# Moving the return of the branches' parts from GpSimd's DMA queue to ScalarE's, one transfer a step

## The chip, the cores and the metric

The kernel runs on one core of a Trainium2 chip. The metric is the device time of one execution in microseconds (us). Three runs of the kernel before gave 2952.59, 2952.63 and 2953.83 us.

## The reference, cut to what matters

Two blocks run one after the other on a sequence of 512 rows of width 1024, in float32. The first is a recurrent layer and a mixture of 32 experts. The second has two layers, each of a feed-forward part, a mixer and another feed-forward part. Only the mixer is touched:

```
p = h @ w_in                                     # h: rmsnorm(x); 512 x (2560 + 3*1024)
gates = sigmoid(p[..., OFF_G:])                  # three gates of width 1024
y_f = fourier_mix(p[..., OFF_F:OFF_B], w_fourier)   # 4 groups of 128 -> 4 x 256
y_c = short_conv(...)                            # 512 -> 1024
y_p = pool_mix(p[..., OFF_P:OFF_G], w_pool, pool_scale)  # 4 groups of 128 -> 4 x 256
merged = gates[0]*y_f + gates[1]*y_c + gates[2]*y_p
x = x + merged @ w_o
```

In `fourier_mix` and in `pool_mix` each of four groups is first transformed along the sequence and then multiplied by a 128 x 256 matrix of its own. The transformed inputs of these products are the branches' parts.

## The kernel before, in words

Every float32 product is three TensorE matmuls (`mm3`, L241 to L243): each operand is a high part in float32r and a low part that holds the rest, and the products are high x high, high x low, low x high. ScalarE writes the high part of a weight block (`whi`, L192), VectorE the low part (`wlo`, L193). Weight blocks are prefetched by SyncE's queue (L157); some get a second block added on the way by an accumulating transfer of GpSimd's queue (L155). `Stream.advance` splits up to four blocks ahead; the tiles `whi` and `wlo` have five buffers each.

The mixer's product with `w_in` is done in groups (`group`), each of seven steps of 24 matmuls with 256 columns. After step i the group calls `todo[i]`, which runs one `tick`; a tick takes every job in the list `jobs` (Python generators) on by one `yield` and starts the new ones, and then `st.advance` prepares more weights. ScalarE reads PSUM after step 0 (L1486), step 1 (L1490), step 2 (L1496) and step 4 (L1505); VectorE reads the banks in `ends` (L1613 after step 3, L1610 after step 5, L1614 and L1615 after step 6). The order on every engine is the order of the program: an instruction that waits holds those behind it on the same engine.

In the first groups of a mixer the transformed inputs are made: `fourier` and `pool` end in `aside`, which splits them into a high and a low part and stores both in HBM (`keep_s`, L1720), as there is no room for them in SBUF. They return later. The last six groups of a mixer are named by g, in the order 4, 2, 3, 0, 1, 5. After each of the groups g = 2, 3, 0 and 1, TensorE does four small products of 512 columns, 12 matmuls, with the weights of `wbranch` and the two parts of group g that have come back: `BR[0]` (pool) and `BR[1]` (Fourier), each with a high and a low tile of 256 KB. The product i uses `BR[i % 2]`. The next group's steps follow on TensorE at once. The job `gates_pf` reads the four banks of the products in the next group (L1822 and L1823), after its steps 3 and 5.

Before the change `branches(g)` runs as one job after step 3 and issues all four transfers from GpSimd (L1838). In groups g = 2 and 3 a further `pool` job starts after step 1. There are four such groups in each of the two mixers, so eight sets of products and 32 transfers.

The tiles of `slot()` have 40 buffers under one tag; the four that a group's parts take are, from the second group on, those of the parts of the group before. In the program that the framework makes, the transfers of the two hardware queues (SyncE's and ScalarE's) share eight completion semaphores in turn, in program order: each waits, on its own engine, until the eighth such transfer before it has landed.

Of the kernel before, what the change touches and what calls it, by code (L numbers as in the profile page):

```python
# [10 lines left out]
F32 = mybir.dt.float32  # L11
# [226 lines left out]
def mm3(nc, ps, w, x, first, last, skip=False):  # L238

    (wh, wl), (xh, xl) = w, x  # L240
    nc.tensor.matmul(ps, wh, xh, start=first, stop=False, skip_group_check=skip)  # L241
    nc.tensor.matmul(ps, wh, xl, start=False, stop=False, skip_group_check=skip)  # L242
    nc.tensor.matmul(ps, wl, xh, start=False, stop=last, skip_group_check=skip)  # L243
# [1017 lines left out]
def dense_phase(K):  # L1261
    tc, A, C, st, X, vc, onesf, ident = (K[n] for n in ("tc", "A", "C", "st", "X", "vc", "onesf", "ident"))
    nc = tc.nc
# [9 lines left out]
    def bank():  # L1273
        return pp.tile([128, 512], F32, name="mm", tag="mm", bufs=6)
# [20 lines left out]
    def tmp(dt=F32):  # L1295
        return stage["pool"].tile([128, S], dt, name="t", tag="t", bufs=NT_F)
# [4 lines left out]
    def slot(x=False):  # L1301

        if x:
            return stage["pool"].tile([128, S], F32R, name="x", tag="x", bufs=4)
        return dp.tile([128, S], F32R, name="s", tag="s", bufs=40)
# [289 lines left out]
    def mixer(l, nxt):  # L1595
        nonlocal h
        keep, keep_s = K["keep"][l], K["keep_s"][l]
# [6 lines left out]
        def line(dt=F32):  # L1604
            return stage["pool"].tile([128, S + 16], dt, name="z", tag="z", bufs=2)
# [11 lines left out]
        def rows(todo, rstd=False, new=wide, margin=0):  # L1617

            t = {}

            def get(r):
                def f(make=False):
                    if make:
                        t[r] = new()
                        if margin:
                            V.memset(t[r][:, :, 0:margin], 0.0)
                            V.memset(t[r][:, :, S + margin:], 0.0)
                    v = t[r][:, :, margin:S + margin] if margin else t[r].rearrange("p (m x) -> p m x", m=2)
                    return v.rearrange("p m (t b) -> p m t b", t=2)
                return f  # L1630
            group(todo, rstd, quarters(get(0), get(1)))
            b = get(1)
            return t, lambda: TT(b()[:, :, 0], b()[:, :, 0], RB[0], op=OP.mult)
# [18 lines left out]
        def steps(**new):  # L1652
            return [lambda i=i: tick(new.get(f"s{i}", ())) for i in range(7)]
# [44 lines left out]
        for g in range(4):  # L1698
# [10 lines left out]
            else:  # L1709
                t = stage["pool"].tile([128, 2, S + 16], F32R, name="L", tag="L", bufs=2)  # L1710
# [5 lines left out]
        def aside(n, src, to=None):  # L1716

            t = yield from split(src, to)
            for i in range(2):
                nc.sync.dma_start(keep_s[2 * n + i], t[i].bitcast(F32))  # L1720
# [33 lines left out]
        def bc(t, i):  # L1754
            TT(t, t, conv[i], op=OP.mult)
            yield
            BC[i] = yield from split(t)

        def pool(t, i, to=None):
            half = 1 << i  # L1760
            w = 2 * half
            up = t[:, i // 2]
            s = [line() for _ in range(2)]
            cur, m = up, 1
            n = 0
            while m < w:
                nx = s[n % 2]
                ln = S + 16 - 2 * m + 1
                TT(nx[:, :ln], cur[:, 0:ln], cur[:, m:m + ln], op=OP.add)
                cur, m, n = nx, 2 * m, n + 1  # L1770
            win = cur[:, 8 - half:8 - half + S]
            yield
            t = tmp()
            act(t, win, AF.Copy, scale=1.0 / w)
            yield
            TT(t[:, 0:half], win[:, 0:half], edge[:, i, 0:half], op=OP.mult)
            if half > 1:
                TT(t[:, S - half + 1:], win[:, S - half + 1:], edge[:, i, 8:8 + half - 1], op=OP.mult)
            TT(t, t, up[:, 8:S + 8], op=OP.subtract)
            yield  # L1780
            yield from aside(4 + i, t, to)

        def once(f):
            f()
            yield 1
# [3 lines left out]
        p, f3 = rows(steps(s0=[once(f2), bc(b[0][:, :S], 0), bc(b[0][:, S:], 2)], s2=[bc(b[1][:, :S], 1)],  # L1789
                           s3=[bc(b[1][:, S:], 3)]), new=lines, margin=8)  # L1790
# [3 lines left out]
        spare = lambda: line(F32R)[:, :S]  # L1794

        def gates_c(t, f, i):

            f()
            act(t[0], t[0], AF.Sigmoid)
            yield  # L1800
            act(t[1], t[1], AF.Sigmoid)
            for r in range(2):
                v = t[r].rearrange("p (m x) -> p m x", m=2)
                if i:
                    nc.sync.dma_start(keep[4 + r:8:2].rearrange("m p x -> p m x"), v)
                    yield
                else:
                    for m in range(2):
                        G[2 * m + r] = v[:, m]

        def gates_pf(t, f, g, ps):

            f()
            act(t[0], t[0], AF.Sigmoid)
            yield
            act(t[1], t[1], AF.Sigmoid)
            yield
            for r in range(2):
                yield
                j = 2 * g + r  # L1820
                u, v = t[r][:, :S], t[r][:, S:]
                STT(u, ps[2 * r], vc("pscale", KD * l + j), u, op0=OP.mult, op1=OP.mult)  # L1822
                TT(v, v, ps[2 * r + 1], op=OP.mult)  # L1823
                if g < 2:
                    if r == 0:
                        Z["t"] = lines()
                    Z[j] = Z["t"][:, r, :S]
                    TT(Z[j], u, v, op=OP.add)
                else:
                    z = tmp()  # L1830
                    TT(z, u, v, op=OP.add)
                    nc.sync.dma_start(keep[8 + j], z)
                yield

        def back(n):
            t = slot(), slot()
            for i in range(2):
                nc.gpsimd.dma_start(t[i].bitcast(F32), keep_s[2 * n + i])  # L1838
            return t

        def load(n):
            g = dp.tile([128, S], F32, name="s", tag="s", bufs=40)
            nc.gpsimd.dma_start(g, keep[n])
            return g

        def loads(j):
            G[j], Z[j] = load(j), load(8 + j)

        BR = {}

        def branches(g):
            BR[0], BR[1] = back(4 + g), back(g)

        new = dict(s0=[once(f3), pool(p[0], 2)], s3=[pool(p[1], 3)])
        for n, g in enumerate((4, 2, 3, 0, 1, 5)):
            if g < 4:
                new["s3"] = [once(lambda: branches(g))]
                if n < 3:
                    new["s1"] = [pool(p[n - 1], n - 1, spare)]
            if g == 5:  # L1860
                loads(4)
                loads(5)
            t, f = rows(steps(**new))
            if g >= 4:
                new = dict(s0=[gates_c(t, f, 5 - g)])
                continue
            w = st.get(h)
            ps = [bank() for _ in range(4)]
            for i in range(4):
                sl = slice(128 * i, 128 * i + 128)  # L1870
                mm3(nc, ps[i], (w[0][:, sl], w[1][:, sl]), BR[i % 2], True, True)
            st.advance(h)
            h += 1
            new = dict(s0=[gates_pf(t, f, g, ps)])
# [109 lines left out]
    for l in range(L2):  # L1984
        ffn(prepper("gmix", l, prep_s), *[None, None] if l else [squares, None, gain("gffn1", 0)])
        close()
        mixer(l, lambda k: prep_s(k, gain("gffn2", l), True))
        if l + 1 < L2:
            ffn(prepper("gffn1", l + 1, prep_s), own=True)
            close()  # L1990
            open_ffn(3)
        else:
            ffn(last, None, tail, own=True)
# [150 lines left out]
```

## Time and profile before

| | |
|---|---|
| three runs, median | 2952.63 us |
| profiled execution | 2954.42 us |
| span of its trace | 2952.6 us |
| mean granted TensorE clock | 0.981 |
| TensorE matmuls busy | 2845.1 us (96% of the span) |
| VectorE busy | 2230.4 us (76%) |
| ScalarE busy | 1657.6 us (56%) |
| GpSimd busy | 403.7 us (14%) |

The profiled execution's time is 1.8 us over its span and 1.8 us over the median of the three runs. TensorE is busy nearly throughout, so a time can only fall where TensorE waits or runs at a lower clock.

### The profile page before, as it was taken

What the parts mean: (1) busy time and instruction counts of PE and PEld (TensorE: products, weight loads), DVE (VectorE), ACT (ScalarE), POOL (GpSimd) and SP (SyncE); (2) the same over time, 40 slices, a digit from 0 to 9 for tenths busy, and PEclk for the clock granted to TensorE, in tenths of its full rate; (3) what the DMA queues carried; (4) which work ended last, traced back from release to release, by engine and by line L of the source; (5) the groups of instructions that cost most, each with busy time, mean ns of one, the idle gap of its engine ahead of it and who ended that gap; (6) DMA issues with size and microseconds to landing.
All of it is one profiled execution on the core that took longest, in us unless ns stands there. A gap on an engine that the chain in (4) does not pass through costs nothing.

```text
span 2952.6 us, 44425 instructions
## 1 busy us (share of the span) xinstructions
PE 2845.1 (96%) x17882; PEld 2471.1 (84%) x17882; DVE 2230.4 (76%) x2778; ACT 1657.6 (56%) x2214; POOL 403.7 (14%) x371
## 2 busy tenths in 40 slices
PE   9997999999889999999899999999999998999998
PEld 7875676667558989998789999899899987899997
DVE  7688888898986758787678667777587876786674
ACT  4746888888764535654356344645356543563442
POOL 0034222220510000101110000100001011100002
PEclk9998999999999999999899999999999999999999
DMA  6374899999943545466644555465454676445551
GB/s 196 123 278 154 336 360 344 369 366 375 358 152 110 157 140 165 137 193 203 198 158 136 156 158 150 131 170 157 137 167 135 192 204 200 158 136 157 157 156 59
DMA packets 113889, 575.04 MB, mean 195 GB/s; under 512 B 13244, under 2 KB 23868, under 8 KB 61328
## 3 DMA queue, kind: packets, MB, share of 16 engines
q1 hardware_dynamic: 87536, 485.31, 44.9%
q0 software_dynamic: 25056, 85.82, 14.6%
q8 instruction: 141, 2.31, 0.3%
q10 hardware_dynamic: 1088, 1.05, 0.1%
q14 instruction: 68, 0.56, 0.1%
HBM read 549.37 MB, written 26.74 MB: 195 GB/s over the span
## 4 chain that ended last, share of the span: by engine, by line
PE 72%; DVE 4%; DMA 4%; ACT 2%; issue 1%; POOL 0%; POOLq 0%; SPq 0%; ACTq 0%; DVEq 0%
PE mm L242 14%; PE mm L243 14%; PE mm L241 14%; PE sv L241 8%; PE sv L243 8%; PE sv L242 8%; PE y L954 3%; DMA s<-branch 2%; DVE wlo L193 2%; PE h L919 2%; PE h L918 2%; ACT whi L192 1%; PE ht L932 1%; DMA rawg<-in_wblocks 1%; PE gat L889 1%
## 5 line engine op out<-in xcount | busy, mean ns | idle before, releaser
L241 PE MATMUL mm<-s,whi 128*128 128x256 f32 (+1 forms) x2262 | 744.6, 329 | 33.6 <-DMA s<-branch 31.4
L193 DVE TENSOR_TENSOR wlo<-raw,whi 128x1024 fp32r<-128x1024 f32 x493 | 606.7, 1240 | 221.5 <-ACT whi L192 221.4
L242 PE MATMUL mm<-s,whi 128*128 128x256 f32 (+1 forms) x2262 | 745.1, 329 | 5.8 <-DMA s<-branch 5.4
L243 PE MATMUL mm<-s,wlo 128*128 128x256 f32 (+1 forms) x2262 | 742.6, 328 | 0.0
L192 ACT ACTIVATE whi<-raw 128x1024 fp32r<-128x1024 f32 x495 | 513.2, 1051 | 156.5 <-PE mm L242 101.3
L241 PE MATMUL sv<-s,whi 128*128 128x256 f32 (+1 forms) x1912 | 544.3, 285 | 1.7 <-ACT sv L1486 1.7
L242 PE MATMUL sv<-s,whi 128*128 128x256 f32 (+1 forms) x1912 | 543.6, 284 | 0.0
L243 PE MATMUL sv<-s,wlo 128*128 128x256 f32 (+1 forms) x1912 | 543.5, 284 | 0.0
L241 PEld LDWEIGHTS mm<-s,whi 128*128 128x128 f32 x2262 | 430.4, 190 | 77.4 <-DMA s<-branch 18.8
L242 PEld LDWEIGHTS mm<-s,whi 128*128 128x128 f32 x2262 | 430.4, 190 | 51.9 <-DMA s<-branch 12.0
L243 PEld LDWEIGHTS mm<-s,wlo 128*128 128x128 f32 x2262 | 430.7, 190 | 38.6
L241 PEld LDWEIGHTS sv<-s,whi 128*128 128x128 f32 x1912 | 359.9, 188 | 4.5 <-ACT sv L1486 2.3
L243 PEld LDWEIGHTS sv<-s,wlo 128*128 128x128 f32 x1912 | 360.0, 188 | 2.2
L242 PEld LDWEIGHTS sv<-s,whi 128*128 128x128 f32 x1912 | 360.0, 188 | 2.1
L193 DVE TENSOR_TENSOR wlo<-rawf,whi 128x1024 fp32r<-128x1024 f32 x158 | 193.6, 1225 | 54.9 <-ACT whi L192 54.9
L193 DVE TENSOR_TENSOR wlo<-rawb,whi 128x1024 fp32r<-128x1024 f32 x162 | 200.1, 1276 | 22.4 <-ACT whi L192 20.3
L1592 DVE SCALAR_TENSOR_TENSOR X<-mm,X 128x512 f32<-128x512 f32 x95 | 65.5, 690 | 189.1 <-PE mm L243 189.0
L919 PE MATMUL h<-wlo,xt 128*64 128x512 f32 x512 | 196.2, 403 | 5.9 <-DVE wlo L193 5.1
L192 ACT ACTIVATE whi<-rawf 128x1024 fp32r<-128x1024 f32 x158 | 165.4, 1049 | 53.0 <-PE mm L242 33.9
L155 POOL DMA_DIRECT2D rawg<-in_wblocks x63 | 54.6, 867 | 986.4 <-DVE wlo L193 433.0
L918 PE MATMUL h<-whi,xt 128*128 128x512 f32 x448 | 181.5, 405 | 6.0 <-PEq L1130 5.0
L1486 ACT ACTIVATE sv<-mm 128x512 f32<-128x512 f32 x63 | 36.6, 582 | 249.2 <-PE mm L243 249.1
(462 smaller groups left out, 4818.0 us busy)
## 6 DMA issues: line engine op xcount, KB each, us to landing
raw<-in_wblocks SPq DMA_DIRECT2D x201, 1024.0 KB, 5.2
rawb<-in_wblocks SPq DMA_DIRECT2D x81, 1024.0 KB, 7.0
rawf<-in_wblocks SPq DMA_DIRECT2D x60, 1024.0 KB, 5.0
rawa<-in_wblocks SPq DMA_DIRECT2D x57, 1024.0 KB, 7.0
rawg<-in_wblocks SPq DMA_DIRECT2D x63, 512.0 KB, 3.6
rawg<-in_wblocks POOLq DMA_DIRECT2D x63, 512.0 KB, 6.9
raw<-in_wblocks POOLq DMA_DIRECT2D x44, 512.0 KB, 5.5
rawf<-in_wblocks POOLq DMA_DIRECT2D x19, 512.0 KB, 5.5
```

The source lines that it names most:

```text
L155: self.nc.gpsimd.dma_start(t[:, x:y], src, accum_op=OP.add)
L192: self.nc.scalar.activation(hi, src, AF.Copy)
L193: f = lambda E=self.nc.vector: E.tensor_tensor(lo, src, hi, op=OP.subtract)
L241: nc.tensor.matmul(ps, wh, xh, start=first, stop=False, skip_group_check=skip)
L242: nc.tensor.matmul(ps, wh, xl, start=False, stop=False, skip_group_check=skip)
L243: nc.tensor.matmul(ps, wl, xh, start=False, stop=last, skip_group_check=skip)
L889: nc.tensor.matmul(ps[:, 256 * v:256 * v + 256], x[c][:, sl], K["oh", g][0][:, c], start=c == 0, stop=c == 3)
L918: nc.tensor.matmul(ps, x, w[0][:, sl], start=k == 0, stop=False)
L919: nc.tensor.matmul(ps[:64], x[:, 0:64], w[1][:, sl], start=False, stop=False)
L954: nc.tensor.matmul(ps[i][:64], hd[:, f, v:v + 64], w[wv][:, sl], start=f == 0 and n == 0, stop=f == 3 and n == 2)
L1486: act(pv, pm, AF.Copy)
L1592: STT(X[j], ps, 0.5, X[j], op0=OP.mult, op1=OP.add)
```

## The change

The helper `back` goes. `branches` becomes a generator: it issues one transfer on ScalarE's queue and yields, four times. It is started after step 1 of the group and not after step 3, ahead of the `pool` job where there is one, so its transfers stand after steps 1, 2, 3 and 4: high and low of the pool part, then high and low of the Fourier part. What is transferred, and between which places, stays as it was.

```
-        def back(n):
-            t = slot(), slot()
-            for i in range(2):
-                nc.gpsimd.dma_start(t[i].bitcast(F32), keep_s[2 * n + i])
-            return t
-
...
         def branches(g):
-            BR[0], BR[1] = back(4 + g), back(g)
+
+            for m in range(2):
+                t = BR[m] = slot(), slot()
+                for i in range(2):
+                    nc.scalar.dma_start(t[i].bitcast(F32), keep_s[2 * (4 - 4 * m + g) + i])
+                    yield
...
             if g < 4:
-                new["s3"] = [once(lambda: branches(g))]
-                if n < 3:
-                    new["s1"] = [pool(p[n - 1], n - 1, spare)]
+                new["s1"] = [branches(g)] + ([pool(p[n - 1], n - 1, spare)] if n < 3 else [])
```

## Rows read from the trace of the kernel before

**Rows 1.** The page, the chain that ended last, by engine.

```profile
PE 72%; DVE 4%; DMA 4%; ACT 2%; issue 1%; POOL 0%; POOLq 0%; SPq 0%; ACTq 0%; DVEq 0%
```

**Rows 2.** Line L1838, the transfers: who waited (us, times), time to landing.

```profile
  PE mm L241: 31.4, 9
...
  PE mm L242: 5.4, 7
...
DMA to landing us min/median/max: 6.8/7.9/12.1
```

**Rows 3.** Windows over TensorE's stops: us; PE, PEld, DVE, ACT, POOL; PEclk; DMA; GB/s.

```profile
1371.55:1384.49 12.94, 5.63 (x13) 3.89 (x14) 8.92 (x11) 2.00 (x2) 3.12 (x6) 0.61 1.02 317
1404.90:1415.09 10.19, 5.53 (x14) 3.79 (x14) 10.09 (x14) 2.00 (x2) 0.90 (x1) 0.68 0.95 315
1435.33:1445.29 9.96, 5.58 (x14) 3.59 (x14) 8.17 (x10) 1.04 (x1) 0.90 (x1) 0.70 0.75 252
1465.77:1472.90 7.13, 4.90 (x14) 3.22 (x13) 7.06 (x9) 1.04 (x1) 1.07 (x2) 0.80 0.27 107
2405.49:2418.26 12.77, 5.61 (x13) 3.89 (x14) 8.67 (x11) 2.00 (x2) 2.91 (x5) 0.63 1.02 318
2438.67:2449.97 11.30, 5.56 (x13) 3.65 (x13) 10.42 (x14) 2.00 (x2) 0.90 (x1) 0.70 0.91 299
2470.07:2480.06 9.99, 5.85 (x12) 3.91 (x13) 8.16 (x10) 1.03 (x1) 0.89 (x1) 0.67 0.96 271
2500.32:2505.46 5.14, 3.59 (x13) 2.28 (x13) 5.11 (x7) 1.03 (x1) 0.47 (x1) 1.00 0.36 143
sum 79.42, PE 42.25 PEld 28.21 DVE 66.60 ACT 12.16 POOL 11.16; mean PE 5.28 PEld 3.53 DVE 8.32 ACT 1.52 POOL 1.39
```

**Rows 4.** Timeline of TensorE, products of the last group of layer 1 (start, us).

```profile
2504.06 0.40 PE L241 MATMUL mm<-s,whi 128*128 128x512 f32 x1
...
2504.99 0.40 PE L242 MATMUL mm<-s,whi 128*128 128x512 f32 x1
```

**Rows 5.** Windows while TensorE never stops, columns as in Rows 3.

```profile
1415.09:1435.33 20.24, 20.24 (x169) 20.04 (x167) 10.97 (x14) 10.62 (x14) 3.06 (x5) 0.99 0.51 139
...
1300.00:1320.00 20.00, 20.00 (x168) 19.87 (x167) 19.39 (x28) 10.94 (x16) 1.73 (x2) 1.00 0.80 222
```

**Rows 6.** Timeline of ScalarE, groups g = 3 and g = 0 of layer 0.

```profile
1393.48 0.58 ACT L1496 ACTIVATE sv<-sv 128x512 f32<-128x512 f32 x1 [0.45 <-PE sv L243]
...
1400.35 0.60 ACT L1505 ACTIVATE t<-sv 128x512 f32<-128x512 f32 x1 [4.29 <-DVE wlo L193]
...
1429.74 0.60 ACT L1505 ACTIVATE t<-sv 128x512 f32<-128x512 f32 x1 [3.63 <-PE sv L243]
```

**Rows 7.** Timeline of GpSimd, group g = 3 of layer 0.

```profile
1398.91 2.53 POOL L1838 DMA_DIRECT2D s<-branch  x4
```

**Rows 8.** Lines of four other transfers: ns min/median/max of an issue, us to landing.

```profile
L1951 ACTq DMA_DIRECT2D outT<-X x4: 378/392/431, 2939.3 to 2945.3; - x4
...
L1720 SPq DMA_DIRECT2D branch<-s x24: 319/402/940, 1281.6 to 2393.7; - x24
...
L1805 SPq DMA_DIRECT2D gates<-T x4: 781/904/1140, 1360.3 to 2397.7; - x4
...
DMA to landing us min/median/max: 7.5/8.0/8.7
...
L1843 POOL DMA_DIRECT2D s<-gates x16: 536/536/543, 1471.7 to 2516.6; - x16
...
DMA to landing us min/median/max: 2.8/3.3/7.5
```

**Rows 9.** Timeline of VectorE, groups g = 2 and g = 3 of layer 0.

```profile
1369.07 0.69 DVE L1613 SCALAR_TENSOR_TENSOR T<-mm,R 128x512 f32<-128x512 f32 x1 [2.30 <-DMA gates<-T]
...
1405.51 0.68 DVE L1823 TENSOR_TENSOR T<-T,mm 128x512 f32<-128x512 f32 x1
...
1409.89 0.68 DVE L1614 TENSOR_TENSOR T<-mm,t 128x512 f32<-128x512 f32 x1
```

## The prediction

> **What bounds the kernel now.** I read the page first: in the chain that ended last TensorE has 72% and transfers 4% [rows 1], so a change to transfers counts where TensorE stops for one. Then the line of these transfers: TensorE's matmuls waited 31.4 + 5.4 = 36.8 us for them, and one takes 7.9 us in the median from issue to landing, up to 12.1 [rows 2]. Then TensorE's timeline at the eight places, which gave the edges of the windows: each begins where the group's last matmul ends and ends with the twelfth product [rows 3]. Together they are 79.42 us. Two things stand in them: the wait, and products at a low clock. The granted clock falls to 0.61 to 0.80 of full speed in seven of the windows, and stays at 1.00, TensorE's upper level of 2.4 GHz, only in the eighth, where the wait is shortest; the others are a mix of that level and the lower one of 1.2 GHz. What the products cost at full speed is seen in that last group, where their matmuls start 0.93 / 4 = 0.23 us apart [rows 4]: 12 x 0.23 = 2.8 us.
>
> So the eight windows hold 79.4 - 8 x 2.8 = 57.0 us that products with their data in place would not need. By window: 10.1, 7.4, 7.2 and 4.3 in layer 0, and 10.0, 8.5, 7.2 and 2.3 in layer 1. That is the upper end of the gain. Between the windows TensorE never stops: 20.24 us for a group's seven steps, 2.9 a step, at a clock of 0.99 [rows 5].
>
> **The change part by part.**
>
> *Taken from GpSimd.* Four issues a group, 2.5 us [rows 7]. GpSimd is busy 3.1 of 20.2 us in such a stretch [rows 5], so I price this at nothing.
>
> *The wait.* The transfers are needed in the order in which they are issued: the first product wants both pool tiles, the second matmul of the second product, 4 x 0.23 = 0.93 us after the start, is the first to want the fourth tile. The first three are now issued after steps 1, 2 and 3; the second, for instance, follows L1496 at 1393.48 [rows 6], 11 us ahead of TensorE's stop at 1404.90 [rows 3]. The longest time to landing was 12.1, with four issued together [rows 2]; I take the first three as landed in time. The fourth decides. It stands behind L1505: in group g = 3 of layer 0 that is 1400.35 + 0.60, and with an issue of 0.39 (ScalarE's own four transfers, at the end of the kernel) 1401.3 [rows 6, 8]. That is no earlier than now, where the four go out from 1398.91 to 1401.44 [rows 7]. It has until 1404.90 + 0.93 = 1405.8, so 4.5 us; in g = 0, from 1430.7 to 1435.33 + 0.93 = 1436.3, so 5.5 us. As all three times hang on TensorE's steps, they keep these distances when the earlier stops go.
>
> How long does it take? The bounds are 2.8, the fastest load of the same 256 KB from HBM, and 12.1, the slowest of these [rows 8, 2]. I take 4: of the rows the gates' loads (median 3.3) are nearest to it, issued one by one, while the 7.9 us belong to four together behind a 512 KB accumulating transfer on the same queue; some more than 3.3 as a 1 MB weight block is in flight at that point. Then the stop goes entirely in the six later groups, and with it the low clock.
>
> *The rule that speaks against it.* The Trainium skill, page "DMA: Bandwidth & Descriptors", section "Issuing engines are not separate DMA queues", says that transfers of all issuing engines run on the same 16 DMA engines and interleave, so that another queue saves only the sequencer's time to issue. By that rule alone the fourth transfer, issued no earlier, would land no earlier; this is the first rival below. The trace shows the engines full in the stops (share 0.75 to 1.02 in six of eight) but half free ahead of them (0.51) [rows 3, 5], and three of the four transfers move into that free part.
>
> *ScalarE.* Four issues a group at 0.39 each; up to 0.94 as SyncE's stores show [rows 8]; below nothing is excluded, since ScalarE only gets more to do. ScalarE is busy 10.6 of 20.2 us [rows 5], so three of them vanish. The fourth stands ahead of the high part of the next group's first block, on which VectorE's tail hangs: VectorE is busy 66.6 of the 79.4 us in the windows [rows 3], working off what the next group's step 1 needs. In g = 3 its L1614 ends at 1410.57 [rows 9] and must end before step 1 writes that bank; without the stop, step 1 would start at 1404.90 + 2.8 + 2.9 = 1410.6. So an issue of 0.39 is seen in full there. L1823, at 1406.19 [rows 9], must also end before the third product, due at 1404.90 + 6 x 0.23 = 1406.3: again some 0.3. I take 1.0 us for each of the two groups g = 3. In g = 0 and g = 1 VectorE has no pool work and some 2 us of room; I take 0.3 each for what I don't see. At 0.94 an issue it is 0.6 more in g = 3, so 1 us in all.
>
> *The first group, g = 2.* Its slots are those of pool parts that are stored only at the start of the same group, and the shared semaphores put the gates' store ahead of the fourth transfer. That store starts at 1360.3, takes up to 8.7 us, and VectorE's L1613 waits for the same one until 1369.07 [rows 8, 9]. With two more transfers in flight (0.5 MB at the 317 GB/s of a full window [rows 3] is 1.6 us, of which part is shared) I put its landing at 1370. ScalarE is held there; behind it are L1658 and the first split of the next group, and VectorE's tail moves by some 2 us, which it can bear since the stop here is 10 us. The fourth transfer goes out at 1370.4 and lands at 1374.4, needed at 1371.55 + 0.93 = 1372.5: a wait of 1.9 us remains, and some of the low clock. What a short wait costs in clock is seen in the fourth window: 7.13 - 2.8 = 4.3 us, of which some 2.4 are waits. I take 1.9 + 1.6 = 3.5 us left in each of the two groups g = 2; bounds 0 and all of the 10.
>
> *The sum.* 57.0 - 2 x 3.5 - 2 x 1.0 - 4 x 0.3 = 46.8 us. Against the profiled execution, 2954.4 - 46.8 = 2907.6; it lies 1.8 us over the median of the runs, so I predict 2906 for the median. Its own range: from 2896 (all 57 us) to 2914 (issues at 0.94, six fourth transfers each 1 us late).
>
> **The rivals.**
>
> *The fourth transfer is late everywhere.* It takes the median 7.9 us after all [rows 2]. It lands at 1409.2 in g = 3 and 1438.6 in g = 0, waits of 3.4 and 2.4 us; with some 2 us of low clock behind each, 5.4 and 4.4, in g = 1 all that the windows hold (4.3 and 2.3). Over both layers 10.8 + 8.8 + 6.6 = 26 us instead of 3.2, so the gain falls to 24: 2929. At 6 us to landing it is about half of that loss, 2918. For it: the issue is no earlier and the engines are shared. Against it: fewer bytes are queued at that moment. Chance 17%.
>
> *ScalarE is held, and the kernel gets slower.* Each transfer waits on ScalarE for an earlier one of the shared semaphores; the high parts of all weights stand behind. If at the fourth transfer of every group ScalarE were held H us, TensorE would lose H less the 2 us of room. It decides from H = 47 / 8 + 2 = 8 us on, a whole median landing; at 10 us it is 8 x 8 - 47 = 17 us slower, 2970. For it: group g = 2 has such a hold, some 2 to 3 us. Against it: in the other groups the eighth transfer before is one of some 15 us ago, and the slots are free since the last products. Chance 5%.
>
> *Nothing changes.* The engines are full in the stops, and if they were the bound of the whole group, earlier issues would only push weights back: 2952.6. Against it: a share of 0.51 between the stops, and a stretch at 0.80 in which TensorE never waits [rows 5]. Chance 5%.
>
> **How the numbers follow.** The forecast has 73%, the rivals 17, 5 and 5. A measurement of this kernel can tell about 0.2%, 6 us, from no change. The forecast and the late fourth transfer are both faster by more: 0.90; nothing changes 0.05; slower 0.05. The range of 8 in 10 takes the forecast's own range and the nearer half of the first rival, up to 2924; its far half, the other two and a tail of the forecast are left out.
>
> **What would show it.** The wait of matmuls for these transfers falls from 36.8 us to some 4, all in the two groups g = 2, and the other six windows shrink to 3 to 4 us at a clock near 1. VectorE takes over as what ends the small stops after the products in g = 3. ScalarE shows one hold of 1 to 3 us ahead of L1658 in each group g = 2. I am wrong if the fourth transfer takes over 6 us to land in the later groups, if an issue costs ScalarE over 1 us, or if TensorE waits for `whi` or `wlo` in the steps after the products by more than 1 us a group.

## The result and the profile after

The changed kernel takes 2910.12 us in the median of three runs (2902.74, 2910.12 and 2920.6) against 2952.63 before: a ratio of 0.9858, 95% interval 0.9809 to 0.9907. Five more runs of the same kernel gave 2903.13 (E1), a ratio of 0.9829 (0.9816 to 0.9843). The forecast was 2906, the range 2896 to 2924. The profiled execution of the changed kernel is the one of 2902.74 us, so its trace shows one of the faster ones.

From its page: the span, and the chain that ended last by engine.

```profile
span 2900.8 us, 44406 instructions
...
PE 69%; DVE 8%; ACT 3%; issue 2%; DMA 2%; POOL 0%; ACTq 0%; DVEq 0%; POOLq 0%; SPq 0%
```

The span is 51.8 us shorter, and the part of transfers in the chain falls from 4% to 2% [rows 1]. The line of the 32 transfers, now L1850 on ScalarE's queue: the first row has min, median and max of an issue in ns, then come those who waited (us, times).

```profile
L1850 ACTq DMA_DIRECT2D s<-branch x32: 326/327/917, 1361.2 to 2447.6; - x32
...
  PE mm L242: 6.2, 4
...
  PE mm L241: 0.2, 1
...
DMA to landing us min/median/max: 2.5/5.6/8.5
```

TensorE's matmuls wait 6.4 us for them where they waited 36.8 [rows 2]. The median landing falls from 7.9 to 5.6 us, the longest from 12.1 to 8.5. The first three became earlier above all: in g = 3 of layer 0 they go out 14.1, 11.2 and 10.8 us ahead of TensorE's stop where it was 6.0, 5.4 and 4.9. The fourth did not. It goes out 4.4 us ahead of the stop both before and after, but lands after 7.3 us and no more after 10.9; in g = 0 of layer 0 its lead is 5.4 us where it was 4.0, and it lands after 2.9 us where it took 10.3. The windows over the same eight sets of products, columns as in [rows 3]:

```profile
1372.37:1376.71 4.34, 3.30 (x14) 2.18 (x13) 4.27 (x6) 2.01 (x2) 0.87 (x1) 1.00 1.04 414
1396.88:1401.86 4.98, 3.07 (x15) 2.18 (x13) 4.91 (x8) 2.00 (x2) 0.87 (x1) 1.00 1.05 252
1421.80:1424.60 2.80, 2.80 (x14) 2.26 (x13) 2.77 (x4) 1.06 (x1) 0.00 (x0) 1.00 1.06 260
1444.53:1447.31 2.78, 2.78 (x15) 2.26 (x13) 2.75 (x4) 1.06 (x1) 0.45 (x1) 1.00 0.64 124
2379.53:2383.10 3.57, 3.05 (x15) 2.19 (x13) 3.54 (x5) 2.01 (x2) 0.87 (x1) 1.00 1.05 429
2403.04:2410.34 7.30, 4.44 (x15) 3.23 (x13) 7.23 (x11) 2.00 (x2) 0.87 (x1) 0.77 1.02 241
2430.28:2433.08 2.80, 2.80 (x14) 2.25 (x13) 2.77 (x4) 1.06 (x1) 0.15 (x1) 1.00 1.02 236
2453.01:2455.79 2.78, 2.78 (x15) 2.26 (x13) 2.75 (x4) 1.06 (x1) 0.46 (x1) 1.00 0.13 25
sum 31.35, PE 25.02 PEld 18.81 DVE 30.97 ACT 12.27 POOL 4.52; mean PE 3.13 PEld 2.35 DVE 3.87 ACT 1.53 POOL 0.57
```

From 79.42 to 31.35 us: 48.1 of the 51.8 us are here. The groups come in the order g = 2, 3, 0, 1. The four windows of g = 0 and 1 are at 2.8 us, the products alone. What is left over 2.8 us is 1.5 and 0.8 in g = 2, and 2.2 and 4.5 in g = 3. The granted clock is 1.00 in seven windows and 0.77 in the slowest. Another 2 us come from the six stretches between the windows of a layer, in which TensorE never stops: here their sums, first after, then before (the first number is the time).

```profile
sum 119.85, PE 119.85 PEld 119.83 DVE 96.33 ACT 63.73 POOL 8.51; mean PE 19.98 PEld 19.97 DVE 16.05 ACT 10.62 POOL 1.42
```

```profile
sum 121.90, PE 121.89 PEld 120.64 DVE 65.98 ACT 63.65 POOL 18.39; mean PE 20.32 PEld 20.11 DVE 11.00 ACT 10.61 POOL 3.06
```

Before, each such stretch ran at a clock of 0.98 to 1.00; after, all at 1.00. The low clock of a stop had reached a little into the steps behind it.

Where the rest of the waits is, TensorE's timeline shows; the bracket is the stop ahead of the matmul and what ended it. Two sets of products, g = 3 of either layer:

```profile
1396.88 0.40 PE L241 MATMUL mm<-s,whi 128*128 128x512 f32 x1
...
1399.89 0.51 PE L242 MATMUL mm<-s,whi 128*128 128x512 f32 x1 [1.91 <-DMA s<-branch]
...
2407.00 0.79 PE L242 MATMUL mm<-s,whi 128*128 128x512 f32 x1 [2.86 <-DMA s<-branch]
```

It is the fifth matmul, the one that wants the fourth tile. The chain of waits gives that transfer's time from issue to landing in the two groups:

```profile
1392.51 7.33 DMA s<-branch
...
2398.80 8.15 DMA s<-branch
```

And ScalarE's timeline, first in g = 2, then in g = 3 of layer 0 (ACTq rows are issues):

```profile
1366.74 0.33 ACTq L1850 DMA_DIRECT2D s<-branch  x1
1367.11 0.63 ACT L192 ACTIVATE whi<-t 128x512 fp32r<-128x512 f32 x1 [1.98 <-DMA branch<-s]
1367.65 0.58 ACT L1505 ACTIVATE t<-sv 128x512 f32<-128x512 f32 x1
1367.99 0.33 ACTq L1850 DMA_DIRECT2D s<-branch  x1
...
1385.62 0.58 ACT L1496 ACTIVATE sv<-sv 128x512 f32<-128x512 f32 x1 [0.45 <-PE sv L243]
1385.64 1.11 ACTq L1850 DMA_DIRECT2D s<-branch  x2
...
1392.49 0.60 ACT L1505 ACTIVATE t<-sv 128x512 f32<-128x512 f32 x1 [4.28 <-DVE wlo L193]
1392.51 0.33 ACTq L1850 DMA_DIRECT2D s<-branch  x1
```

In g = 3 the second and the third transfer go out together at 1385.64, right behind L1496, and the fourth 7 us later, right behind L1505. On ScalarE "four steps" are thus in truth two places: ahead of L1505 and behind it.

Why were the transfers late before? The chain of waits of the kernel before, group g = 3 of layer 0, adds what the prediction only touched:

```profile
1394.32 3.47 DMA rawg<-in_wblocks
...
1398.38 0.50 POOL rawg L155
1398.91 0.47 POOL s L1838
1399.46 10.52 DMA s<-branch
```

GpSimd's accumulating transfer into `rawg` (L155) may go only when SyncE's load of the same tile has landed; GpSimd waits there until 1398.4, with the four transfers behind it. In all eight groups that wait ends within 0.1 us of the load's landing.

### The profile page after: what moved, and what is told of

Same layout as the page of the kernel before. It is cut to its first block, busy times and chain, and to the rows that moved or that the text cites. A ratio compares the mean times of both kernels' runs of the same rounds, so it can differ in the third digit from the quotient of the medians.

```text
span 2900.8 us, 44406 instructions
## 1 busy us (share of the span) xinstructions
PE 2824.2 (97%) x17882; PEld 2457.3 (85%) x17882; DVE 2231.0 (77%) x2778; ACT 1658.3 (57%) x2214; POOL 390.9 (13%) x339
## 4 chain that ended last, share of the span: by engine, by line
PE 69%; DVE 8%; ACT 3%; issue 2%; DMA 2%; POOL 0%; ACTq 0%; DVEq 0%; POOLq 0%; SPq 0%
PE mm L242 13%; PE mm L243 13%; PE mm L241 13%; PE sv L241 7%; PE sv L243 7%; PE sv L242 7%; DVE wlo L193 4%; PE y L954 2%; PE h L919 2%; ACT whi L192 2%; PE h L918 1%; DMA s<-branch 1%; PE ht L932 1%; PE gat L889 1%; DVE raw L198 1%
## 5 line engine op out<-in xcount | busy, mean ns | idle before, releaser
L155 POOL DMA_DIRECT2D rawg<-in_wblocks x63 | 54.6, 867 | 960.1 <-DVE wlo L193 530.2
L954 PE MATMUL y<-whi,hd 128*64 128x512 f32 x512 | 161.5, 397 | 2.5 <-ACT whi L192 1.5
```

The source lines that it names most:

```text
L155: self.nc.gpsimd.dma_start(t[:, x:y], src, accum_op=OP.add)
L954: nc.tensor.matmul(ps[i][:64], hd[:, f, v:v + 64], w[wv][:, sl], start=f == 0 and n == 0, stop=f == 3 and n == 2)
```

## The experiments

Theory: the gain comes from what stands ahead of the four issues on the issuing engine. On GpSimd that is L155, which waits for a load; on ScalarE it is an ACTIVATE. What is left of the waits comes from the fourth transfer behind L1505. Rival theories: it is the spreading over four steps that helps, or the kind of queue (GpSimd's transfers being the slower ones once issued). All times in us; the waits are those of TensorE's matmuls for `s<-branch` in the trace. Kernels timed together share a median of the kernel before: E1 to E4 2953.69, E5 to E8 2956.68, E9 2954.99.

| | kernel | median (lowest to highest) | ratio to before (95%) | waits |
|---|---|---|---|---|
| E1 | after, again | 2903.13 (2900.2 to 2906.8) | 0.9829 (0.9816 to 0.9843) | 8.3 |
| E2 | before, ScalarE's queue | 2897.88 (2894.6 to 2898.7) | 0.9809 (0.9796 to 0.9823) | 2.2 |
| E3 | after, GpSimd's queue | 2978.12 (2974.2 to 2982.3) | 1.0086 (1.0071 to 1.0101) | 59.4 |
| E4 | after, products 0, 2, 1, 3 | 2904.08 (2895.8 to 2910.2) | 0.9826 (0.9812 to 0.9839) | 10.9 |
| E5 | after, in three steps | 2898.58 (2896.4 to 2898.9) | 0.9799 (0.9786 to 0.9811) | 0.8 |
| E6 | GpSimd, all four after step 1 | 2910.39 (2905.4 to 2911.6) | 0.9836 (0.9824 to 0.9849) | 9.1 |
| E7 | no transfers | 2894.67 (2893.8 to 2896.1) | 0.9790 (0.9776 to 0.9804) | 0 |
| E8 | after, fourth a step later | 2913.02 (2906.9 to 2919.8) | 0.9858 (0.9844 to 0.9873) | 9.4 |
| E9 | before, SyncE's queue | 2919.80 (2916.6 to 2922.7) | 0.9876 (0.9859 to 0.9892) | 12.9 |

One further execution of E6 took 12,234 us; it stands outside the range given, and its cause is open.

**E1, the changed kernel unchanged.** 

> The changed kernel as it is, once more, as its three runs lay 18 us apart where those of before lay 1 us apart. Theory A (what is left of the waits for the fourth tile decides, and each wait is short, so a transfer that lands 1 us later costs up to 3 us with the clock behind it): the runs scatter between 2900 and 2922 us again, and a profile of a slower run shows longer waits of TensorE for these transfers than the 6.4 us in the profile so far, in the groups g = 2 and g = 3. Theory B (the scatter comes from elsewhere): a slower run shows the same 6 to 7 us of these waits, and its loss in another stretch.

Measured: 2903.13. It puts the size of the change at 50.6 us, with runs 6.6 us apart. Its profiled execution is no slower one than the first (2903.13 against 2902.74 us) and has 8.3 us of these waits where the first had 6.4, so this run does not decide between the two theories.

**E2, the queue alone.** The kernel before with one word changed; all four still follow step 3.

```
-                nc.gpsimd.dma_start(t[i].bitcast(F32), keep_s[2 * n + i])
+                nc.scalar.dma_start(t[i].bitcast(F32), keep_s[2 * n + i])
```

> The kernel before with one word changed: all four transfers still go after step 3 as one job, but from ScalarE's queue. Theory A (the time of issue against the time of need decides, and GpSimd's issues are late since they stand behind an accumulating weight transfer that waits for its first half): on ScalarE the four go out right after the split that follows L1496, some 8 us ahead of the products, none behind L1505, so nearly all of the gain comes: 2896 to 2912 us. Theory C (starting two steps earlier is what brings the gain): the start is the same step as before, so a small part comes at most: 2935 to 2953 us.

Measured: 2897.88, a gain of 55.8 us; each of its runs is faster than each of E1's on the same chip. So the change of queue alone brings the whole gain, and the change's new places take some 5 us of it back. ScalarE's timeline in g = 3 of layer 0 shows why:

```profile
1384.78 0.58 ACT L1496 ACTIVATE sv<-sv 128x512 f32<-128x512 f32 x1 [0.42 <-PE sv L243]
1384.92 0.33 ACTq L1838 DMA_DIRECT2D s<-branch  x1
...
1385.98 0.95 ACTq L1838 DMA_DIRECT2D s<-branch  x2
...
1391.65 0.60 ACT L1505 ACTIVATE t<-sv 128x512 f32<-128x512 f32 x1 [4.04 <-DVE wlo L193]
```

Though the program issues them after step 3, ScalarE need not wait for step 3 to do so: they go out behind L1496, which reads step 2, the last of them 5 us ahead of L1505. The median landing is 5.8 us, no faster than in the change.

**E3, the steps alone.** The change with GpSimd's queue in place of ScalarE's.

```
-                    nc.scalar.dma_start(t[i].bitcast(F32), keep_s[2 * (4 - 4 * m + g) + i])
+                    nc.gpsimd.dma_start(t[i].bitcast(F32), keep_s[2 * (4 - 4 * m + g) + i])
```

> The changed kernel with the transfers left on GpSimd's queue, one after each of the steps 1 to 4. Theory A: the first goes early, but the second already stands behind the accumulating weight transfer of the same queue, so three go out about when they do in the kernel before; the fewer bytes at once bring 5 to 20 us: 2933 to 2948 us. Theory C: the start after step 1 brings the gain whatever the queue: 2900 to 2915 us.

Measured: 2978.12, slower than before by 0.86%, which neither theory had forecast. GpSimd's timeline (g = 0 of layer 0), then the chain of waits there:

```profile
1435.51 0.90 POOL L155 DMA_DIRECT2D rawg<-in_wblocks  x1 [14.33 <-DVE t L1831]
1436.07 1.44 POOL L1850 DMA_DIRECT2D s<-branch  x2
1446.92 0.89 POOL L155 DMA_DIRECT2D raw<-in_wblocks  x1 [9.41 <-DMA raw<-in_wblocks]
1447.48 0.90 POOL L1850 DMA_DIRECT2D s<-branch  x1
```

```profile
1437.05 9.32 DMA raw<-in_wblocks
...
1447.48 5.53 DMA s<-branch
```

The groups g = 2, 3 and 0 have a second accumulating transfer, between the third and the fourth of the four. It waits for a load of 1 MB that takes 9.3 us, and the fourth transfer, a step later than before, now stands behind that one too. The theory holds, and is stronger than I had it: the same four steps gain 50 us on one engine and lose 24 on another.

**E4, another order of the products.** `for i in (0, 2, 1, 3)` in place of `range(4)`: the two products of the pool part come first, so that the fourth tile is wanted three matmuls, 0.7 us, later.

> The changed kernel with the four products in the order 0, 2, 1, 3, so that both products of the pool part come first and the fourth tile is first needed after 7 matmuls instead of 4, 0.7 us later. Theory A: each of the short waits left shrinks by up to 0.7 us and the clock behind it stays up more often: 2 to 8 us faster than the changed kernel run beside it, with less scatter. Theory B (these waits are not what scatters): within 2 us of it, with the same scatter. The third product's bank is freed late by VectorE in the groups g = 3, which can take 0.3 us of it back.

Measured: 2904.08, not to be told from E1; its runs lie 14 us apart, so the 2 to 8 us and the smaller scatter of theory A did not come. Theory B's reason did not either: the profiled execution is the slowest of the five (2910.17), and has waits of 10.9 us. That 0.7 us is too little beside a landing that took from 2.5 to 9.4 us here is argued, not shown.

**E5, the fourth ahead of L1505.** Two transfers after step 1 and one after each of steps 2 and 3.

```
-                    yield
+                    if m or i:
+                        yield
```

> The changed kernel with the transfers moved up: two after step 1, one after step 2, one after step 3, so that none stands behind L1505. Theory A (what separates the changed kernel from the one with the queue alone is the fourth transfer's place behind L1505 and behind the weights issued at that point): the waits in the groups g = 3 go, 2894 to 2900 us, level with the run of the queue alone. Rival D (the rest is due to spreading over several steps, which holds ScalarE more often): it stays at 2902 to 2910 us.

Measured: 2898.58, waits of 0.8 us. The landings are no shorter than in the change (median 5.6, up to 9.0 us). In g = 3 of layer 0 the first three go out within 1.6 us of where they did, and the fourth at 1386.29 and no more at 1392.51. With every issue ahead of that one ACTIVATE the change has what it still lacked, as E2 has it in another way.

**E6, GpSimd's queue, early enough.** All four on GpSimd in one go after step 1: `nc.gpsimd`, and one `yield` behind the four.

> All four transfers on GpSimd's queue as before, as one job, but after step 1, which in GpSimd's order is ahead of the accumulating transfer of the weights. Theory A (what stood ahead of the transfers in the queue was the fault of the kernel before, not the kind of queue): they go out as soon as the slots are free, 15 us ahead of the products in the later groups, and the gain comes as well: 2893 to 2905 us. Rival E (GpSimd's software queue itself makes them slow, 7.9 us against some 6 on ScalarE's): with so early a start it also comes in time, so only waits in the groups g = 2 would tell, some 2 us each. If the queue is what counts however early the issue, 2930 to 2953 us.

Measured: 2910.39, 5 us above the range given for theory A. GpSimd's timeline, g = 2 and the next group of layer 0:

```profile
1370.23 1.06 POOL L1850 DMA_DIRECT2D s<-branch  x2 [11.85 <-DMA branch<-s]
1373.14 0.89 POOL L155 DMA_DIRECT2D rawg<-in_wblocks  x1 [1.84 <-DMA rawg<-in_wblocks]
...
1380.82 1.12 POOL L1850 DMA_DIRECT2D s<-branch  x2 [1.27 <-PE mm L242]
1382.09 1.07 POOL L1850 DMA_DIRECT2D s<-branch  x2
1396.81 0.90 POOL L155 DMA_DIRECT2D rawg<-in_wblocks  x1 [13.64 <-DVE T L1823]
```

From the second group on the four go out 11 us or more ahead of the L155 into `rawg`, behind which they stood before, and no matmul waits for them. All 9.1 us of waits are in the two groups g = 2, where GpSimd is held by the stores of the pool part until 1370. These two windows are 10.4 and 9.0 us long, the other six 2.8: what E6 lacks against E5 is there. So GpSimd's queue serves too, 46 us faster than before, if the issue stands ahead of that wait. The kind of queue does not make the gain.

**E7, the ceiling.** No transfers: the products read two other tiles that are already in SBUF. This leaves out 8 MB of loads and their issues, and computes the products with other data.

> No transfers at all: the products read two pairs of tiles that are always in SBUF (those of the short convolution), so the products are computed with other data and the 8 MB of loads are left out. It is the ceiling. Theory A: all that the windows of the kernel before hold is the wait and its clock, 57 us, less some 0 to 3 us in which TensorE then waits for VectorE: 2894 to 2899 us. Rival F (the freed engines and slots bring more, or another wait takes a part of the 57 us back): below 2891 or above 2903 us.

Measured: 2894.67, 62.0 us under before; the span of its trace is 60.2 us shorter, near the 57.0 that the windows were said to hold. E5, on the same chip, is 3.9 us above it: about that much is all that 32 issues on ScalarE, the traffic and the 0.8 us of waits left cost together.

**E8, the fourth later still.** One more `yield` ahead of the fourth transfer.

> The changed kernel with the fourth transfer alone one tick later, after step 5, behind one more convert and one or two splits on ScalarE, some 2 us later. Theory A: each of the eight places has 0 to 2 us of room and loses the rest and up to 2 us of clock: TensorE's waits for these transfers rise from some 7 to 15 to 22 us, and the time to 2912 to 2932 us. Rival D: the fourth one's place does not matter, 2900 to 2908 us.

Measured: 2913.02 with runs 13 us apart, and waits of 9.4 us in its (fastest) profiled execution, where 15 to 22 were expected. But the edit did not move the issue. ScalarE's timeline in g = 3 of layer 0:

```profile
1390.49 0.60 ACT L1505 ACTIVATE t<-sv 128x512 f32<-128x512 f32 x1 [4.29 <-DVE wlo L193]
1390.57 0.33 ACTq L1852 DMA_DIRECT2D s<-branch  x1
```

The fourth transfer still goes out right behind L1505, 4.2 us ahead of the first product (1394.75) where it was 4.4; in seven of the eight groups its lead is that of the change within 0.2 us. One more `yield` makes a place in the program, and on ScalarE it is the same place. So E8 says nothing of a later issue. Its median is 10 us over E1's, but its ratio of 0.9858 is also that of the first three runs of the change, and its runs lie within the eight of the change (2900.2 to 2920.6).

**E9, SyncE's queue at the old place.** As E2, with `nc.sync`.

> The kernel before with the four transfers s<-branch issued on SyncE after step 3, where GpSimd issued them; nothing else is changed. In the kernel before, SyncE issues the weights of the next part, then the gates' store, which waits for VectorE, and GpSimd issued the four at 1398.91 us behind the accumulating weight transfer. On SyncE the four stand behind the gates' store, so they are issued at about 1399 us in the g=3 group, no earlier than by GpSimd. Theory (what counts is what stands ahead in the queue that issues): they are still late in most groups, the waits for them sum to 12 to 35 us in the trace, and the time is 2910 to 2945 us. Rival (the kind of queue counts, GpSimd's software-fed one being the slow one): they land within 4 us of issue, the waits sum to under 8 us, and the time is 2896 to 2906 us, as with ScalarE's queue.

Measured: 2919.80, waits of 12.9 us. The chain of waits, g = 3 of layer 0:

```profile
1394.06 0.20 SPq L1832
...
1394.36 0.38 SPq L1838
...
1395.80 7.09 DMA s<-branch
```

The issues stand behind the gates' store, as expected. In absolute time they are 4.6 us earlier than the 1399 that I gave, since the group g = 2 lost much of its stop; against TensorE's own stop they are nearly where GpSimd's were (5.5 us ahead of 1399.9; before, 1398.91 to 1404.90 is 6.0). The rival falls: the line's median landing is 7.2 us, not under 4, on a hardware queue. The 35 us that are gained have two sources. Half of what the windows lose, 15 of 31 us, is in g = 2, where SyncE issues 6.8 and 6.5 us ahead of TensorE's stop and GpSimd issued 0.3 and 0.5 us ahead of it (1371.29 in layer 0):

```profile
1366.67 3.15 SPq L1838 DMA_DIRECT2D s<-branch  x4
```

In g = 3 the lead is nearly the same, and the four land in 6.7 to 8.3 us instead of 8.7 to 12.1. What is away there is L155 directly ahead; that this is the reason, and not the kind of queue, is argued, not shown.

## Why the prediction was right, point by point

**The size of the hole** held: 57.0 us in the windows, 60.2 in the trace without transfers (E7). The rest is in part the steps behind the stops, where the clock came back late: 2.05 us after the change.

**The sum** came out because two errors cancel. What was to remain, and what the windows after show:

| us left over 2.8 in the windows | forecast | measured |
|---|---|---|
| g = 2, two groups | 7.0 | 2.3 |
| g = 3, two groups | 2.0 | 6.7 |
| g = 0 and 1, four groups | 1.2 | 0.0 |
| gain in the windows | 46.8 | 48.1 |

**"I take 4", the fourth transfer's landing**, is the term that was mis-sized. It held in g = 0 and 1 (2.9, 5.2, 3.7 and 3.2 us). In g = 3 it took 7.3 and 8.2 us, near the median of the four together that I had set aside; to take over 6 us in the later groups was one of the prediction's own signs of being wrong. The first rival (late fourth) thus holds in g = 3: it gave waits of 3.4 us, the rows show 1.9 and 2.9. In g = 0 and 1 nothing waits in this trace. That the sum came out all the same is luck.

The share of the DMA engines does not tell the late ones from the others: over the fourth transfer's flight it is 0.97 and 0.99 in g = 3, and 0.84 to 1.00 in g = 0 and 1. The order of two issues does, in the two traces of this kernel. In g = 3 SyncE's load of a 1 MB weight block goes out 0.7 us ahead of the fourth transfer. In g = 0 of layer 1 it went out 0.06 us behind it; in E1's trace of the same kernel it went out 0.07 us ahead, the fourth took 7.8 us and not 3.7, and TensorE waited 1.4 us. The issues in the change, then in E1, there with the chain of waits for the transfer:

```profile
2424.92 0.35 ACTq L1850 DMA_DIRECT2D s<-branch  x1
2424.98 0.42 SPq L157 DMA_DIRECT2D raw<-in_wblocks  x1
```

```profile
2423.52 0.40 SPq L157 DMA_DIRECT2D raw<-in_wblocks  x1
...
2423.59 7.84 DMA s<-branch
```

The prediction had seen that block ("a 1 MB weight block is in flight at that point") and gave it 0.7 us. In E4 one more is late in g = 0, at 6.6 us, behind an L155 of GpSimd. No run changes this order alone, so as a cause it is not shown.

**VectorE as what ends the small stops in g = 3** does not show in the changed kernel: in TensorE's timeline of layer 0 the twelfth product is followed by the next group's first matmul 0.23 us later. There the late fourth transfer hides it. Where that one is in time, TensorE does wait for L1614 in the two groups g = 3, as the prediction said; in E5, for instance (us in total, times, longest):

```profile
PE mm L241 <- DVE T L1614: 1.2, 2, 0.9
```

In E2 and in E7 it is 0.3 us in each of the two. So the path was right and 1.0 us for each group too much; and as E7 has no issues on ScalarE, these 0.3 us are not the price of an issue.

**The first group, g = 2.** The hold on ScalarE was there, 1.98 us in layer 0, but ahead of the third transfer, and for the stores of the pool part, not for the gates' store. So the fourth went out at 1368.0 and not at 1370.4. It landed shortly before 1374.8 where 1374.4 was forecast: a hold taken too long and a landing taken too short. The low clock that I added there did not come: after a wait of 0.9 us the window is at 1.00, even after 1.9 us (g = 3 of layer 0); after 2.9 us it is at 0.77, with products 0.43 us apart instead of 0.23.

**Issues at 0.39 us** were 0.33 in the median. The rival "ScalarE is held" has rows in g = 2 alone, and its price of 8 us a group was never near. One such hold does reach TensorE: in E5, g = 2 of layer 1, ScalarE waits 4.5 us for the pool part's stores, and TensorE 1.1 us for L1505 behind it.

**Taken from GpSimd, priced at nothing**, was true for the work, but it was the wrong question. Nothing was lost on GpSimd, but what stood ahead of the transfers there was the cause of most of the wait (E2, E6). The prediction looked for when the four would be issued, and found the fourth "no earlier than now"; it did not ask why they were issued so late now.

**The rule of the Trainium skill** (page "DMA: Bandwidth & Descriptors", section "Issuing engines are not separate DMA queues"): transfers of all engines share 16 DMA engines, and another queue saves only issuing time. Once issued, the rows agree roughly: median landings of 7.9 (GpSimd, before), 7.2 (SyncE, E9), 6.6 (GpSimd, E6) and 5.8 us (ScalarE, E2). For the kernel the conclusion does not hold: the choice of queue alone is worth 55.8 us, since an issue waits its turn on its engine. And the fourth transfer of g = 3 in layer 0, issued no earlier, did land earlier: 3.6 us sooner after its issue.

**The scatter.** The kernels with the fourth transfer behind L1505 (the change twice, E4, E8) have runs 7 to 18 us apart, those with all four ahead of it (E2, E5) or with none (E7) 2 to 4 us, and in their traces the span goes with the waits, nearly throughout: 2892.4 us at none, 2896.9 at 0.8 us, 2895.6 at 2.2, 2900.8 at 6.4, 2901.2 at 8.3, 2905.0 at 9.4, 2908.2 at 10.9. A transfer that is just in time or just late passes its own variation on. That the run of 2920.6 us is of this kind is likely; it has no trace, so it stays open.

## What to carry to other kernels

Ahead of a late transfer, ask first what stands before its issue on the engine that issues it, and what that waits for; an accumulating transfer that waits for its base load holds everything behind it. An engine is free of the program's steps where its own instructions are: put the issue behind the last instruction that it must wait for anyhow, and not a step later for the sake of an even spread. Where it really goes out, the trace tells and the program does not (E2, E8). Where the slack is about the landing time, give it a landing time more: the runs then also agree better.

## What the runs showed of the hardware

The same 256 KB load from HBM took from 2.5 to 8.5 us to land within one execution of the changed kernel, and up to 10.6 in E9. At one and the same place of the changed kernel it took 3.7 us in one execution and 7.8 in another, with the issue of a 1 MB load 0.06 us behind it or 0.07 us ahead. I had not expected a single transfer to take as long as one of four, nor GpSimd's spread issues to make the kernel 24 us slower.
